# Transposing the second layer's sixteen softmax weights in SBUF: VectorE's 32x32 blocks and GpSimd copies

## The chip, the cores and the metric

The kernel runs on one core of a Trainium2 chip. The metric is the device time of one execution in microseconds (us), lower is better. Times are medians over several executions; where lines of a profile are shown, they come from one profiled execution.

## What is computed

The reference is an encoder trunk of two layers (DEPTH = 2) over 256 tokens of 2048 channels, all in float32. Each layer has a mixer and a gated feed-forward part with a short convolution. The mixer projects the normalised input to the q, k, v of two attention branches of eight heads each, head size 128. Branch A is attention with a window of +-128 tokens, two key/value groups and a learned sink; branch B is attention over neighbours in a 64-wide token grid with a learned bias table. What matters here is, for each of the sixteen heads of a layer:

```python
s = jnp.einsum('bnqgrd,bnkgd->bgrnqk', qb, kw) * (HEAD_DIM ** -0.5)   # scores (mask and sink, or bias, follow)
p = jnp.exp(s - m)
p = p / (jnp.sum(p, axis=-1, keepdims=True) + jnp.exp(snk - m))       # softmax weights
o = jnp.einsum('bgrnqk,bnkgd->bnqgrd', p, vw)                        # weights times values
```

The weights p of one head are a matrix of 256 queries by 256 keys. The scores come out with the queries on the 128 partitions (two tiles t of 128 queries); the product with the values needs the keys on the partitions (two tiles of 128 keys). So p has to be transposed between the softmax and the product.

## The kernel before, in words

**The weight stream.** Nearly all of TensorE's time goes into products with weight matrices. Each layer's weights are one long stream of 128x128 blocks, in units of 16 (1 MB). `unit_steps` (L319 on) loads a unit by a DMA of SP into one of four `raw` buffers, then splits it in two halves of 8 blocks: ScalarE casts to a rounded high part (L336), VectorE subtracts for the low part (L337), into one of four `hl` buffers. TensorE multiplies each block three times: high by high, high by low, low by high (L355 to L357 with features on the partitions, L418 to L420 with tokens on the partitions). The values and p are split in the same way by `split` (L427 on: cast at L430, subtract at L431).

**What runs beside it.** At the end of each unit `Stream.tick` calls `bg.tick`, which advances background jobs by a rate in steps per unit, and `plan`, which issues the loads and reductions (L231, L232) for the modulation of later parts. The attention of a layer is such a job: `attention()` keeps a list of live heads; each step advances every live head by one stage and then starts the next head, if its q, k and v are ready. The rate is `ATT[l]` from the end of the third group of the input projection, and in layer 1 `ATT_B[1]` = 0.4 from the end of branch A's output projection. `attended(HA)`, ahead of that projection, and `bg.finish(job)`, ahead of branch B's, run what is left at once.

**A head.** `head_a` and `head_b` start a head: q and k are split in halves in layer 1 (`SCORES_3`), and branch B takes a buffer p and loads the head's bias into it (SP, L889). `attend` (L643 on) is the rest, a stage up to each `yield`: the score matmuls (L648), the mask or bias addition with the row maximum (L651, into p), the exponential and the scaling (L659, L667); then the transpose and the split into pT, which has one buffer; then the product po with the values (L697) and its split into the head's output (L699, L700). The buffers p are two.

**The transpose, in two ways.** `rows` is None in layer 0 and in layer 1's branch A: TensorE transposes four 128x128 tiles into PSUM (L689) and `split` reads them there. In layer 1's branch B (`MOVED[1]` = (0, 8)) `turned_blocks` is called: VectorE transposes the 32x32 blocks of each query tile within themselves (L313), four DMAs of GpSimd for each tile put the blocks in their places in DRAM (L316), and two DMAs of SP read the transposed matrix back (L299), over the q and k of the head, which nobody needs any more. The reads are queued some units later (`BACK`), behind a VectorE instruction of the stream (`halved`, a dependency by hand). Two empty stages give all this time, so such a head has six stages and the others have four.

Instructions are issued in an order that a scheduler works out when the program is built, with the program's order as priority; an engine then takes them strictly in that order.

Of the kernel before, what the change touches and what calls it, by code (L numbers as in the profile page):

```python
# [9 lines left out]
F32 = mybir.dt.float32  # L10
F32R = mybir.dt.float32r
AF = mybir.ActivationFunctionType
ALU = mybir.AluOpType
AX = mybir.AxisListType

P = 128
# [10 lines left out]
EPS = 1e-6  # L27
NEG = -1e30
SCALE = HEAD ** -0.5
BEHIND = mybir.DependencyInfo(mybir.DependencyClass.Sync, mybir.DependencyReason.DATA)  # L30
GRID_W, NA_KH, NA_KW = 64, 8, 16
BLOCK = 32

# [46 lines left out]

H_RATE = [2.7, 1.7]

ATT = [1.288, 0.4]
ATT_B = [0.21, 0.4]

SCORES_3 = (1,)

BACK = [3, 4]
MOVED = [(0, 0), (0, 8)]

ADA_ORDER = [[p * KC + k for k in range(KC) for p in ps] for ps in ((0, 1), (2,), (3, 4), (5,))]
ADA_ORDER = [i for part in ADA_ORDER for i in part]
# [47 lines left out]
def encoder(ctx: ExitStack, tc: tile.TileContext, a: dict, out: bass.AP):  # L140
# [16 lines left out]
    sm = pool("sm", 3)  # L157
    mm = pool("mm", 4, space=bass.MemoryType.PSUM)
    ax = pool("ax", 3, space=bass.MemoryType.PSUM)
    dram = pool("dram", 2, space=bass.MemoryType.DRAM)  # L160

    ident = const.tile([P, P], F32, name="ident")
    make_identity(nc, ident[:])
# [43 lines left out]
    def paired(dt, name):  # L207

        t = ev.tile([P, 2 * S + ROW], dt, name=name, tag="u", bufs=2)
        return t[:, ROW - OFF : ROW - OFF + 2 * S].rearrange("p (a s) -> p a s", a=2)  # L210
# [71 lines left out]
                pass  # L282

    bg = Paced()
    halved = [None]

    def once(fn):

        due = [fn]

        def run():
            if due:
                due.pop()()

        return run

    def read_back(dst, src):

        tc.add_manual_dep(nc.sync.dma_start(dst, src).ins, halved[0], BEHIND)  # L299

    def later(n, fn):

        if n == 0:
            fn()
        else:
            bg.defer(lambda: later(n - 1, fn))

    def turned_blocks(p, rows, n, tag):

        y = dram.tile([P, n, S], F32, name=tag, tag=tag)  # L310
        to = y[:].rearrange("(b i) n (t a j) -> t a i n b j", i=BLOCK, t=2, a=P // BLOCK)
        for t, row in enumerate(rows):
            nc.vector.transpose(out=row, in_=p[t])  # L313
            src = row.rearrange("p (n b j) -> p n b j", n=n, j=BLOCK)
            for a in range(P // BLOCK):
                nc.gpsimd.dma_start(to[t, a], src[a * BLOCK : (a + 1) * BLOCK])  # L316
        return y

    def unit_steps(l, u, by_halves=False):  # L319

        raw = rawp.tile([P, UB * P], F32, name=f"w{l}_{u}", tag="raw")
        if not by_halves:
            nc.sync.dma_start(raw[:], a["ws"][l, u])
        halves = []
        streamed = any(m == "w_in" and mo < GATE_A // P for m, _, mo in STREAMS[l][u * UB : (u + 1) * UB])
        at = OFF if streamed else 0
        for j in range(2):
            n = UB * P // 2  # L330
            hl = hlp.tile([P, 2 * n + ROW], F32R, name=f"hl{l}_{u}_{j}", tag="hl")
            hl = hl[:, at : at + 2 * n].rearrange("p (a n) -> p a n", a=2)
            r = raw[:, j * n : (j + 1) * n]
            if by_halves:
                nc.sync.dma_start(r, a["ws"][l, u][:, j * n : (j + 1) * n])
            nc.scalar.copy(hl[:, 0], r)  # L336
            halved[0] = nc.vector.tensor_tensor(  # L337
                out=hl[:, 1], in0=r, in1=hl[:, 0].bitcast(F32), op=ALU.subtract
            ).ins.name
            halves.append(hl)  # L340
            if j == 0:
                yield halves
# [300 lines left out]
    def attend(q, k, v, p, mask, scale, sink, o, rows=None):  # L643

        sc = ax.tile([P, 2, S], F32, name="sc", tag="ax")
        for t in range(2):
            for i, j in by(q):
                nc.tensor.matmul(sc[:, t], q[i][:, t * P : (t + 1) * P], k[j], start=i + j == 0, stop=(i, j) == by(q)[-1])  # L648
        m = sm.tile([P, 2], F32, name="m", tag="m")
        for t in range(2):  # L650
            nc.vector.tensor_tensor_reduce(  # L651
                out=p[:, t], in0=sc[:, t], in1=mask[:, t], scale=scale, scalar=-3.0e38 if sink is None else sink,
                op0=ALU.add, op1=ALU.max, accum_out=m[:, t : t + 1],
            )
        nm = sm.tile([P, 2], F32, name="nm", tag="nm")
        nc.vector.tensor_scalar(out=nm[:], in0=m[:], scalar1=-1.0, scalar2=None, op0=ALU.mult)
        den = sm.tile([P, 2], F32, name="den", tag="den")
        for t in range(2):
            nc.scalar.activation(out=p[:, t], in_=p[:, t], func=AF.Exp, bias=nm[:, t : t + 1], accum_out=den[:, t : t + 1])  # L659
        if sink is not None:  # L660
            es = sm.tile([P, 2], F32, name="es", tag="es")
            nc.scalar.activation(out=es[:], in_=nm[:], func=AF.Exp, bias=sink)
            nc.vector.tensor_tensor(out=den[:], in0=den[:], in1=es[:], op=ALU.add)
        ri = sm.tile([P, 2], F32, name="ri", tag="ri")
        nc.vector.reciprocal(out=ri[:], in_=den[:])
        for t in range(2):
            nc.scalar.activation(out=p[:, t], in_=p[:, t], func=AF.Copy, scale=ri[:, t : t + 1])  # L667
        yield
        if rows is not None:
            rows = rows()  # L670
            y = turned_blocks([p[:, t] for t in range(2)], rows, 2, "pY")

            def back():
                for k in range(2):
                    read_back(rows[k], y[:, k])

            back = once(back)
            later(BACK[sink is None], back)
            yield
            yield  # L680
            back()
            pT = at.tile([P, 2, 2, S], F32R, name="pT", tag="pT", bufs=1)
            for k in range(2):
                split(pT[:, :, k], rows[k])
        else:
            tp = ax.tile([P, 2, S], F32, name="tp", tag="ax")
            for k in range(2):
                for t in range(2):
                    nc.tensor.transpose(tp[:, k, t * P : (t + 1) * P], p[:, t, k * P : (k + 1) * P], ident[:])  # L689
            pT = at.tile([P, 2, 2, S], F32R, name="pT", tag="pT", bufs=1)  # L690
            split(pT, tp[:])
        v = v()
        yield
        po = ax.tile([P, 512], F32, name="po", tag="ax")
        for i, j in by(v):
            for b in range(2):
                nc.tensor.matmul(po[:, :S], v[i][:, b], pT[:, j, b], start=i + j + b == 0, stop=i + b == 2)  # L697
        o = o()
        nc.scalar.copy(o[:, 0], po[:, :S])  # L699
        nc.vector.tensor_tensor(out=o[:, 1], in0=po[:, :S], in1=o[:, 0].bitcast(F32), op=ALU.subtract)  # L700
# [115 lines left out]
    for l in range(L):  # L816
# [41 lines left out]
        def head_a(i):  # L858
            g = i // (HA // GA)
            if i >= 6:  # L860
                oA.append(paired(F32R, f"oA{l}_{i}"))
            elif i % 2 == 0:
                o = place(("y0", "y1", "y2")[i // 2], 4, F32R, f"oA{l}_{i}")
                oA.extend((o[:, :2], o[:, 2:]))
            q = in_halves(qTa[:, i], f"qA{l}_{i}", "qh", l in SCORES_3)
            if i % (HA // GA) == 0:
                kvs[0] = in_halves(kTa[:, g], f"kA{l}_{g}", "kh", l in SCORES_3)
            k = kvs[0]
            yield
            p = at.tile([P, 2, S], F32, name="p", tag="p")  # L870

            def v():
                if i % (HA // GA) == 0:
                    kvs[1] = in_halves(packs[0][:, 1:4:2, g * HEAD : (g + 1) * HEAD], f"vA{l}_{g}", "vh", True)
                return kvs[1]

            def rows():
                spare = ev.tile([P, S], F32, name=f"spare{l}_{i}", tag="r", bufs=2)
                return [qTa[:, i], spare[:]]

            yield from attend(
                q, k, v, p, tables[0], SCALE, sink[:, i : i + 1], lambda: oA[i], rows if i < MOVED[l][0] else None
            )

        def head_b(hb):
            b, i = packs[1 + hb // 4], hb % 4
            v = b[:, 4:8].rearrange("p (t a) s -> p t (a s)", t=2)
            p = at.tile([P, 2, S], F32, name="p", tag="p")
            nc.sync.dma_start(p[:], a["bias"][l, hb])  # L889
            q = in_halves(b[:, 8 + i], f"qB{l}_{hb}", "qh", l in SCORES_3)  # L890
            k = in_halves(b[:, i], f"kB{l}_{hb}", "kh", l in SCORES_3)
            yield
            yield from attend(
                q, k, lambda: in_halves(v[:, :, i * HEAD : (i + 1) * HEAD], f"vB{l}_{hb}", "vh", True), p, p, 1.0, None,
                lambda: oB_of(hb), (lambda: [b[:, 8 + i], b[:, i]]) if hb < MOVED[l][1] else None,
            )

        def oB_of(hb):
# [314 lines left out]
```

## Time and profile before

| | |
|---|---|
| median of 3 runs | 2661.03 us (2660.66 to 2664.07) |
| profiled execution | 2661.44 us |
| its span, first to last instruction | 2659.3 us |
| busy: TensorE, VectorE, ScalarE, GpSimd | 2647.6, 2106.2, 1411.5, 75.0 us |
| DMA | 704.63 MB, mean 265 GB/s |

Busy time counts an engine's instructions, without the time in which it waits or issues DMAs. TensorE's matmuls overlap one another, so their single durations add up to more than the time they take: it is better to look at the distance from start to start, or at the chain of work that ended last. Two layers follow one another; layer 1's attention lies at about 1500 to 1800 us. In the profile's lines `ps_t` is the output of a product with tokens on the partitions, `ps` of one with features on the partitions, `tp` the transposed p in PSUM, `pY` the matrix in DRAM.

### The profile page before, as it was taken

The numbers are of one execution on the slowest core, as the hardware profiler recorded it, in microseconds if no ns is written. First come the engines' busy times: TensorE is split into PE (matmuls) and PEld (weight loads), VectorE is DVE, ScalarE is ACT, GpSimd is POOL, SyncE is SP. The second block draws the span as 40 slices with busy tenths as digits, with TensorE's granted clock in tenths as the row PEclk, the third lists the DMA queues.
The fourth block names the chain that finished last, engine by engine and source line by source line (L and its number), as shares of the span: only waits on it lengthen the run. The fifth ranks groups of instructions, "written<-read, shape, count | busy, mean of one in ns | idle before, by whom it ended". The sixth has DMA issues, their size and how long they took to land.

```text
span 2659.3 us, 50973 instructions
## 1 busy us (share of the span) xinstructions
PE 2647.6 (100%) x21224; PEld 2562.6 (96%) x21224; DVE 2106.2 (79%) x2983; ACT 1411.5 (53%) x2292; POOL 75.0 (3%) x89
## 2 busy tenths in 40 slices
PE   9999999999999999999999999999999999999999
PEld 7888899999999999999998889999999999999999
DVE  8898998997987888788876666868888866655664
ACT  5445865456653554355554566555565445544553
POOL 0001100000000000000000001310000000000000
PEclk9999999999999999999999999999999999999999
DMA  9987789885777778788756666877747765555554
GB/s 365 349 327 297 264 300 351 321 311 212 290 295 286 296 290 287 288 297 296 295 205 256 236 229 238 299 264 261 278 179 287 297 251 191 191 197 194 196 191 143
DMA packets 106394, 704.63 MB, mean 265 GB/s; under 512 B 14001, under 2 KB 18353, under 8 KB 22321
## 3 DMA queue, kind: packets, MB, share of 16 engines
q1 hardware_dynamic: 104114, 699.27, 71.6%
q8 instruction: 166, 2.72, 0.4%
q0 software_dynamic: 2048, 2.10, 0.3%
q14 instruction: 66, 0.54, 0.1%
HBM read 697.13 MB, written 4.19 MB: 264 GB/s over the span
## 4 chain that ended last, share of the span: by engine, by line
PE 90%; DVE 5%; DMA 2%; ACT 1%; issue 1%; POOL 0%; DVEq 0%; ACTq 0%
PE ps L355 25%; PE ps L357 25%; PE ps L356 25%; PE ps_t L420 4%; PE ps_t L418 4%; PE ps_t L419 4%; DVE hl L337 2%; DVE aw L232 1%; DMA aw<-in_aw 1%; PE sc L648 1%; PE po L697 1%; ACT hl L336 1%; PE tp L689 0%; PE qtp L621 0%; DMA w<-in_ws 0%
## 5 line engine op out<-in xcount | busy, mean ns | idle before, releaser
L337 DVE TENSOR_TENSOR hl<-w,hl 128x1024 fp32r<-128x1024 f32 x928 | 1128.4, 1222 | 338.7 <-ACT hl L336 332.1
L336 ACT CAST hl<-w 128x1024 fp32r<-128x1024 f32 x928 | 970.6, 1049 | 738.3 <-PE ps L357 509.5
L355 PE MATMUL ps<-h,hl 128*128 128x256 f32 x3328 | 923.9, 278 | 1.3 <-DVE ya L979 0.6
L356 PE MATMUL ps<-h,hl 128*128 128x256 f32 x3328 | 921.1, 277 | 0.0
L357 PE MATMUL ps<-h,hl 128*128 128x256 f32 x3328 | 920.9, 277 | 0.0
L355 PEld LDWEIGHTS ps<-h,hl 128*128 128x128 f32 x3328 | 625.0, 188 | 2.4 <-DVE ya L979 0.8
L356 PEld LDWEIGHTS ps<-h,hl 128*128 128x128 f32 x3328 | 625.6, 188 | 0.4
L357 PEld LDWEIGHTS ps<-h,hl 128*128 128x128 f32 x3328 | 624.6, 188 | 0.0
L232 DVE CUSTOM_DVE_ANT_0 aw<-aw,cact,ab 128x2048 f32<-128x2048 f32 x189 | 443.5, 2347 | 61.1 <-DMA aw<-in_aw 60.4
L418 PE MATMUL ps_t<-hl,h 128*128 128x512 f32 x576 | 223.5, 393 | 2.1 <-ACT h L510 1.6
L419 PE MATMUL ps_t<-hl,h 128*128 128x512 f32 x576 | 225.1, 391 | 0.4
L420 PE MATMUL ps_t<-hl,h 128*128 128x512 f32 x576 | 224.6, 391 | 0.0
L1058 DVE SCALAR_TENSOR_TENSOR u<-ps,cw,u 128x255 f32<-128x255 f32 x304 | 146.2, 481 | 66.5 <-ACT u L1056 62.5
L1056 ACT ACTIVATE u<-ps,cw 128x256 f32<-128x256 f32 x152 | 85.7, 564 | 183.1 <-PE ps L357 183.0
L357 PE MATMUL ps<-merged,hl 128*128 128x256 f32 x512 | 141.8, 277 | 0.2 <-DVE hl L337 0.2
L355 PE MATMUL ps<-merged,hl 128*128 128x256 f32 x512 | 141.7, 277 | 0.0
L356 PE MATMUL ps<-merged,hl 128*128 128x256 f32 x512 | 141.7, 277 | 0.0
L356 PE MATMUL ps<-act_o,hl 128*128 128x256 f32 x512 | 141.6, 277 | 0.0
L357 PE MATMUL ps<-act_o,hl 128*128 128x256 f32 x512 | 141.6, 276 | 0.0
L355 PE MATMUL ps<-act_o,hl 128*128 128x256 f32 x512 | 141.4, 277 | 0.0
L418 PEld LDWEIGHTS ps_t<-hl,h 128*128 128x128 f32 x576 | 108.0, 188 | 25.5 <-ACT h L510 2.6
L419 PEld LDWEIGHTS ps_t<-hl,h 128*128 128x128 f32 x576 | 108.2, 188 | 24.0 <-DVE hl L337 2.1
(235 smaller groups left out, 4657.8 us busy)
## 6 DMA issues: line engine op xcount, KB each, us to landing
w<-in_ws SPq DMA_DIRECT2D x463, 1024.0 KB, 5.0
aw<-in_aw SPq DMA_DIRECT2D x189, 1024.0 KB, 6.1
p<-in_bias SPq DMA_DIRECT2D x16, 256.0 KB, 4.4
x<-in_xT SPq DMA_DIRECT2D x4, 512.0 KB, 5.5
aw_o<-in_aw SPq DMA_DIRECT2D x2, 1024.0 KB, 13.1
pY<-packB POOLq DMA_DIRECT2D x64, 32.0 KB, 4.2
packB<-pY SPq DMA_DIRECT2D x16, 128.0 KB, 2.7
out<-x SPq DMA_DIRECT2D x16, 128.0 KB, 2.6
```

The costliest lines, as they stand in the source:

```text
L232: nc.vector.tensor_tensor_reduce(out=raw[:], in0=raw[:], in1=cact[:], scale=1.0, scalar=ab[:, i : i + 1], op0=ALU.mult, op1=ALU.add, accum ...
L336: nc.scalar.copy(hl[:, 0], r)
L337: halved[0] = nc.vector.tensor_tensor(out=hl[:, 1], in0=r, in1=hl[:, 0].bitcast(F32), op=ALU.subtract).ins.name
L355: nc.tensor.matmul(out, hi, act[0], start=first, stop=False)
L356: nc.tensor.matmul(ps[:, :S], hi, act[1], start=False, stop=False)
L357: nc.tensor.matmul(out, lo, act[0], start=False, stop=last)
L418: nc.tensor.matmul(ps[:], xh, hi, start=kc == kcs[0], stop=False)
L419: nc.tensor.matmul(ps[:], xh, lo, start=False, stop=False)
L420: nc.tensor.matmul(ps[:], xl, hi, start=False, stop=kc == kcs[-1])
L648: nc.tensor.matmul(sc[:, t], q[i][:, t * P : (t + 1) * P], k[j], start=i + j == 0, stop=(i, j) == by(q)[-1])
L1056: nc.scalar.activation(out=u, in_=ps, func=AF.Identity, scale=w[:, 1:2], bias=w[:, 3:4])
L1058: nc.vector.scalar_tensor_tensor(out=u[:, to], in0=ps[:, of], scalar=w[:, j : j + 1], in1=u[:, to], op0=ALU.mult, op1=ALU.add)
```

## The change

In layer 1 all sixteen heads now go through `turned_blocks`, and it no longer uses DRAM. VectorE transposes the 32x32 blocks of both query tiles in one instruction (128 x 512), from p into `rows`. Then sixteen copies by GpSimd, each of 32 partitions by 2 x 2 x 32 elements, take the blocks from partition group b to partition group a, back into p, which then holds the transposed matrix. `split` reads it from p in one cast and one subtract of 512 elements, as it reads PSUM in layer 0. The stages that a head waits between the copies and the split are `STEPS` (one for each branch), so each head of layer 1 has five stages. For branch A `rows` is the q of this head and of the one before it (for head 0 a spare buffer), for branch B the head's k and q as before. The rate of layer 1's attention goes from 0.4 to 0.43 steps a unit (`ATT`). The DRAM buffers, the read-backs, `BACK`, `once` and the dependency by hand go. Layer 0 keeps TensorE's transposes.

```diff
-ATT = [1.288, 0.4]
+ATT = [1.288, 0.43]
...
-BACK = [3, 4]
-MOVED = [(0, 0), (0, 8)]
+MOVED = [(0,0), (8,8)]
+STEPS = [1, 1]
...
-    def turned_blocks(p, rows, n, tag):
-
-        y = dram.tile([P, n, S], F32, name=tag, tag=tag)
-        to = y[:].rearrange("(b i) n (t a j) -> t a i n b j", i=BLOCK, t=2, a=P // BLOCK)
-        for t, row in enumerate(rows):
-            nc.vector.transpose(out=row, in_=p[t])
-            src = row.rearrange("p (n b j) -> p n b j", n=n, j=BLOCK)
-            for a in range(P // BLOCK):
-                nc.gpsimd.dma_start(to[t, a], src[a * BLOCK : (a + 1) * BLOCK])
-        return y
+    def turned_blocks(src, rows, n):
+
+        nc.vector.transpose(out=rows, in_=src)
+        blocks = rows.rearrange("p t (n k) -> p n t k", n=n)
+        dst = src.rearrange("p t (n k) -> p (t n k)", n=n).rearrange("p (n t k) -> p n t k", n=n, t=2)
+        for b in range(0, P, BLOCK):
+            for a in range(0, P, BLOCK):
+                nc.gpsimd.tensor_copy(
+                    out=dst[a : a + BLOCK, :, :, b : b + BLOCK], in_=blocks[b : b + BLOCK, :, :, a : a + BLOCK]
+                )
...
         if rows is not None:
-            rows = rows()
-            y = turned_blocks([p[:, t] for t in range(2)], rows, 2, "pY")
-
-            def back():
-                for k in range(2):
-                    read_back(rows[k], y[:, k])
-
-            back = once(back)
-            later(BACK[sink is None], back)
-            yield
-            yield
-            back()
-            pT = at.tile([P, 2, 2, S], F32R, name="pT", tag="pT", bufs=1)
-            for k in range(2):
-                split(pT[:, :, k], rows[k])
+            turned_blocks(p[:], rows(), 2)
+            for _ in range(STEPS[sink is None]):
+                yield
+            tp = p
         else:
...
-            pT = at.tile([P, 2, 2, S], F32R, name="pT", tag="pT", bufs=1)
-            split(pT, tp[:])
+        pT = at.tile([P, 2, 2, S], F32R, name="pT", tag="pT", bufs=1)
+        split(pT, tp[:])
...
             def rows():
-                spare = ev.tile([P, S], F32, name=f"spare{l}_{i}", tag="r", bufs=2)
-                return [qTa[:, i], spare[:]]
+                return qTa[:, i - 1 : i + 1] if i else paired(F32, f"spare{l}")
...
-                lambda: oB_of(hb), (lambda: [b[:, 8 + i], b[:, i]]) if hb < MOVED[l][1] else None,
+                lambda: oB_of(hb), (lambda: b[:, i : 9 + i : 8]) if hb < MOVED[l][1] else None,
```

More of the change, by code (lines that the diff above doesn't have):

```diff
@@ L29 @@
 SCALE = HEAD ** -0.5
-BEHIND = mybir.DependencyInfo(mybir.DependencyClass.Sync, mybir.DependencyReason.DATA)
 GRID_W, NA_KH, NA_KW = 64, 8, 16
@@ L159, in encoder @@
     ax = pool("ax", 3, space=bass.MemoryType.PSUM)
-    dram = pool("dram", 2, space=bass.MemoryType.DRAM)
     ident = const.tile([P, P], F32, name="ident")
@@ L284, in encoder @@
     bg = Paced()
[L285 to L299, printed above, removed]
     def later(n, fn):
@@ L336, in unit_steps @@
             nc.scalar.copy(hl[:, 0], r)
-            halved[0] = nc.vector.tensor_tensor(
-                out=hl[:, 1], in0=r, in1=hl[:, 0].bitcast(F32), op=ALU.subtract
-            ).ins.name
+            nc.vector.tensor_tensor(out=hl[:, 1], in0=r, in1=hl[:, 0].bitcast(F32), op=ALU.subtract)
             halves.append(hl)
```

## The prediction

> **What bounds the kernel now.** I read the page first: the span, the busy times, the chain that ended last.
>
> ```profile
> span 2659.3 us, 50973 instructions
> ...
> PE 2647.6 (100%) x21224; PEld 2562.6 (96%) x21224; DVE 2106.2 (79%) x2983; ACT 1411.5 (53%) x2292; POOL 75.0 (3%) x89
> ...
> PE 90%; DVE 5%; DMA 2%; ACT 1%; issue 1%; POOL 0%; DVEq 0%; ACTq 0%
> ```
>
> TensorE is busy all the time and 90% of the chain. A busy TensorE need not be dense, so I went on to the windows of the second layer's attention (branch A about 1500 to 1640 us, branch B 1640 to 1760) and to TensorE's waits from 1400 to 1850 us, where the only one listed is this:
>
> ```profile
> 1500.00:1640.00 140.00, 139.94 (x814) 123.02 (x813) 95.47 (x161) 90.56 (x199) 4.91 (x3) 1.00 0.64 234
> 1640.00:1760.00 120.00, 120.00 (x1053) 120.00 (x1053) 93.85 (x169) 70.02 (x132) 39.37 (x64) 1.00 0.80 279
> ```
> ```profile
> PEld tp L689 <- ACT packB L622: 0.3, 1, 0.3
> ```
>
> The columns after the length are TensorE, weight loads, VectorE, ScalarE, GpSimd, granted clock, DMA share and GB/s. TensorE has no stall to give back here beyond 0.3 us, also in branch B, where the weights go through DRAM. The clock is full. So the change gains only what it takes off TensorE, and loses only what makes TensorE wait.
>
> How much lateness of VectorE and ScalarE stays unseen? Two rows of TensorE's timeline, 24 matmuls apart, and ScalarE's rows for branch A:
>
> ```profile
> 1628.79 0.28 PE L357 MATMUL ps<-h,hl 128*128 128x256 f32 x1
> ...
> 1631.51 0.28 PE L357 MATMUL ps<-h,hl 128*128 128x256 f32 x1
> ```
> ```profile
> L336 ACT CAST hl<-w 128x1024 fp32r<-128x1024 f32 x44 | 45.9, 1046 | 35.8 <-PE ps_t L420 32.5 <-PE ps L357 3.3
> ```
>
> Half a unit of weights (8 blocks, 24 matmuls) lasts 2.72 us. ScalarE idles 35.8 us before the casts because TensorE has not yet freed an hl buffer: there are four. A freed buffer is wanted again three halves later (8.2 us); refilling it takes 1.05 us on ScalarE and 1.22 us on VectorE (L337, below). So the weights lead by an estimated 5.9 us, and a hold-up shorter than that costs nothing.
>
> **What goes from TensorE.** In branch A of layer 1, eight heads times four transposes:
>
> ```profile
> L689 PE MATMUL tp<-ident,p x32: 270/272/327, 1519.2 to 1634.2; 128*128 128x128 f32 x32
> ```
> ```profile
> 1569.55 0.44 PE tp L689 x4
> ...
> 1633.78 0.66 PE tp L689 x4
> ```
>
> The 272 ns overlap one another; in the chain a group of four costs 0.44 us, and 0.66 us only where it also waited for ScalarE. 8 x 0.44 = **3.5 us**; the upper bound is 8 x 0.66 + 0.3 = 5.6 us, the lower 8 x 0.27 = 2.2 us, if of each group only one transpose counted. I take 3.5, since seven of the eight groups stand in the chain with 0.44. Branch B has none of these (its eight heads go by DRAM already), so it gains nothing on TensorE.
>
> **VectorE and ScalarE.** By line, for the two windows:
>
> ```profile
> L337 DVE TENSOR_TENSOR hl<-w,hl 128x1024 fp32r<-128x1024 f32 x45 | 54.4, 1223 | 28.4 <-ACT hl L336 28.3
> L232 DVE CUSTOM_DVE_ANT_0 aw<-aw,cact,ab 128x2048 f32<-128x2048 f32 x7 | 16.4, 2349 | 6.1 <-DMA aw<-in_aw 6.1
> ...
> L431 DVE TENSOR_TENSOR pT<-tp,pT 128x512 fp32r<-128x512 f32 x8 | 5.5, 684 | 0.1
> ...
> L431 DVE TENSOR_TENSOR qA<-packA,qA 128x256 fp32r<-128x256 f32 x7 | 3.0, 422 | 0.0
> ```
> ```profile
> L337 DVE TENSOR_TENSOR hl<-w,hl 128x1024 fp32r<-128x1024 f32 x41 | 50.0, 1221 | 19.6 <-ACT hl L336 15.5 <-PE sc L648 4.0
> L232 DVE CUSTOM_DVE_ANT_0 aw<-aw,cact,ab 128x2048 f32<-128x2048 f32 x7 | 16.4, 2342 | 1.3 <-DMA aw<-in_aw 1.2
> ...
> L313 DVE STREAM_TRANSPOSE packB<-p 128x256 f32<-128x256 f32 x16 | 6.4, 430 | 1.7 <-ACT p L667 1.7
> ...
> L431 DVE TENSOR_TENSOR pT<-packB,pT 128x256 fp32r<-128x256 f32 x12 | 4.5, 419 | 0.0
> L431 DVE TENSOR_TENSOR qB<-packB,qB 128x256 fp32r<-128x256 f32 x6 | 2.5, 423 | 0.0
> L431 DVE TENSOR_TENSOR vB<-packB,vB 128x256 fp32r<-128x256 f32 x6 | 2.5, 420 | 0.0
> L431 DVE TENSOR_TENSOR kB<-packB,kB 128x256 fp32r<-128x256 f32 x6 | 2.5, 419 | 0.0
> ```
>
> 256 more elements cost 0.684 - 0.419 = 0.27 us, so a block transpose of 512 is an estimated 0.43 + 0.27 = 0.70 us. Branch A gains eight: 5.6 us over 140 in which VectorE is 68% busy (95.47); the idle time before L337 hides them. Branch B replaces 2 x 0.43 by 0.70 and, in the subtract into pT, 2 x 0.42 by about 0.68: 0.3 us less a head. ScalarE:
>
> ```profile
> L430 ACT CAST pT<-packB x16: 406/417/420, 1662.9 to 1783.2; 128x256 fp32r<-128x256 f32 x16
> L430 ACT CAST pT<-tp x8: 577/592/616, 1520.4 to 1634.5; 128x512 fp32r<-128x512 f32 x8
> ```
>
> One cast of 512 replaces one in branch A (0.59 us, now from SBUF) and two of 256 in branch B (0.83): nothing, or 0.2 us less a head, on an engine at 65% and 58%. All of it is off the path: 0.
>
> **GpSimd.** It loses 64 DMA issues and gets 16 heads x 16 copies of 32 partitions x 128 elements. No copy of this kind is in the trace. The nearest rows:
>
> ```profile
> L316 POOL DMA_DIRECT2D pY<-packB x64 | 39.4, 618 | 96.6 <-DVE packB L313 51.8 <-issue 44.4
> ...
> masks.py:199 POOL TENSOR_SCALAR_AFFINE_SELECT ident<-ident 128x128 f32<-128x128 f32 x1 | 0.3, 292 | 0.1
> masks.py:197 POOL MEMSET ident<- 128x128 f32 x1 | 0.2, 204 | 0.3 <-POOLq L1205 0.3
> ```
>
> The select reads and writes 128 elements a partition, as a copy does, so I take its 0.29 us: 4.7 us a head. Bounds: 0.20 (the memset, which reads nothing) and 0.62 us (a DMA issue), 3.3 to 9.9 us a head.
>
> Time for them: the 32 transposes of L689 span 115 us for eight heads, 16.4 us a head at 0.4 steps a unit (2.5 units), so 15.2 us at 0.43. In branch B the score matmuls lie
>
> ```profile
> 1634.56 0.77 PE sc L648 x6
> ...
> 1735.63 0.68 PE sc L648 x6
> ```
>
> seven heads apart: 14.4 us each. Between the block transposes, which follow the softmax, and the split stand two or three units, and pT has one buffer, which the head before frees only with its own po. So 4.7 us fit, even stretched to 10.
>
> The fifth stage that branch A gets (four before) needs the higher rate: head 7 starts about unit 41 of the layer instead of 43 and ends at 51 instead of 50; line `attended(HA)` forces the rest only at 52. Nothing is forced: 0.
>
> **VectorE against GpSimd.** The trace has one clear meeting of the two, first GpSimd's power, once disturbed and once not, then VectorE's timeline:
>
> ```profile
> 259.13 4.08 POOL L482 TENSOR_TENSOR qrs<-qss,mhalf 128x8 f32<-128x8 f32 x1 [8.03 <-DVE qss L481]
> ...
> 1563.45 1.64 POOL L482 TENSOR_TENSOR qrs<-qss,mhalf 128x8 f32<-128x8 f32 x1 [26.63 <-DVE qss L481]
> ```
> ```profile
> 258.96 0.29 DVE L613 TENSOR_TENSOR qn<-rt 128x128 f32<-128x128 f32 x1
> ...
> 259.36 2.36 DVE L337 TENSOR_TENSOR hl<-w,hl 128x1024 fp32r<-128x1024 f32 x2
> 261.63 1.29 DVE L949 TENSOR_TENSOR packB<-ps_t,packB 128x512 f32<-128x512 f32 x2
> ```
>
> The power ends at 263.21, 1.58 us after VectorE's last instruction with both inputs in SBUF gave way to one that reads PSUM: GpSimd stood still for 2.5 us, and the two L337 lasted 2.36 us, as always. So copies pass between VectorE's two-SBUF-input instructions. These (L337, L232, qA) fill 73.8 of 140 us in branch A, with the new subtract from SBUF 8.7 of 15.2 us a head, which leaves 6.5 us, 0.41 a copy. In branch B (L337, L232, pT, qB, vB, kB) they fill 78.4 of 120, 9.4 of 14.4 us a head: 5.0 left, **0.31 a copy**. At 0.29 it fits, narrowly in branch B.
>
> The Trainium skill, "SBUF — State Buffer", section "Who interferes with whom", says that a VectorE instruction with two SBUF inputs contends with a GpSimd instruction that reads SBUF, and that the second to issue blocks until the first ends; the row at 259.13 agrees on GpSimd's side, and no row shows VectorE held. The skill's "GPSIMD Engine Reference", section 3.1, gives about 1.8 cycles an element at 1.2 GHz in a good loop, by which a copy would be an estimated 0.19 us and a head 3.1 us; no run here shows it, and the sum would be the same.
>
> **DMA queues.** The 64 stores and 16 read-backs go, with SP's wait on them: nothing waits for SP that TensorE feels, so 0. But p now lives until the split, and there are two p buffers. A branch-B head loads its bias into p when it starts, and adds the scores to it one step later. So far the load waits for the block transposes of the head two before; now it waits for that head's split, which stands in the very step of the addition:
>
> ```profile
> SPq L889 <- DVE packB L313: 18.7, 5, 5.6
> ```
> ```profile
> DMA to landing us min/median/max: 2.4/4.0/5.5
> ```
>
> (The second row is from p's own view, layer 1: from a bias load's issue to its landing.) Behind it on SP stand the weight loads, with four raw buffers (some 22 us) ahead; behind the mask addition that wants it on VectorE stand L337s, with 5.9 us. A load of 4.0 us fits into that, and the head's own block transposes aren't due before the next step: 0.
>
> **Sum.** The profiled execution took 2661.44 us (span 2659.3 and 2.1 around it), 0.4 above the median of 2661.03. 2661.4 - 3.5 = **2657.9**, less 0.13%. About 0.2% (5.3 us) is what a measurement of this kernel can tell from no change, so this counts as within.
>
> **The rivals.**
> - *The copies run into VectorE (slower).* For: 0.31 us of room a copy in branch B against 0.29. Against: VectorE wasn't held in the one meeting. It decides from 0.31 us in branch B, 0.41 in A. At 0.45, midway between the select and the DMA issue, 16 copies are 7.2 us: B overruns by 9.4 + 7.2 - 14.4 = 2.2, A by 0.7; eight heads each: 23 - 3.5, so 2681. At 0.62 it is about 2723. Chance 0.22.
> - *The bias comes late.* For: VectorE takes its instructions in order, and the addition stands close behind the split that lets the load go. If it waits for the whole landing and the subtracts of pT, qB, kB and vB (0.68 + 3 x 0.42 = 1.9 us) stand with it, the lead of 5.9 us just covers a landing of 4.0 us and is 1.5 us short at 5.5; four of the eight heads at 5.5 cost 6 us, so 2664. Against: other work can be put between split and addition. Chance 0.12.
> - *Nothing is gained*, since the new order of VectorE's work costs the 3.5 us elsewhere: 2661.4. Chance 0.05.
> - *All of the transposes' waits go too*, by the upper bound 5.6 us: 2655.8 or less. Chance 0.04.
>
> **How the numbers follow.** The forecast has 0.57. Within 0.2%: 0.57 + 0.12 + 0.05 = 0.74; slower 0.22; faster 0.04. The range starts at 2656, just above the best case, and ends at 2674, a copy of 0.42 us (B overruns by 1.7, A by 0.2, 8 x 1.9 - 3.5 = 12); above it I leave out the worse half of the first rival.
>
> **What would show it.** Right: no tp in layer 1; TensorE's waits from 1480 to 1800 us still under 1 us; copies at 0.2 to 0.3 us each, a head's sixteen done within 10 us; L337 at 1.22 us. Wrong: po or ps waiting for VectorE or ScalarE there; a pT cast waiting for GpSimd; a mask addition waiting for the bias for over 3 us; L337 longer than 1.3 us, which would mean that GpSimd holds VectorE.

## The result, and the profile after

The changed kernel takes 2659.41 us (median of 22 executions, 2656.18 to 2663.97) against 2664.14 us for the kernel before, run beside it (22, 2660.66 to 2676.13): ratio 0.998, 95% interval 0.9972 to 0.9988, that is 3.2 to 7.5 us less. The forecast, 3.5 us less (0.9987), lies inside; as a time it was 2657.9 us, 1.5 below the median. In three later comparisons the kernel before took 2661.0, 2660.9 and 2661.5 us, so part of the 4.7 us between the medians is scatter.

Where that scatter is, and what the change does without it, two rows of TensorE show. The first is the first matmul of layer 1 with tokens on the partitions, ahead of all attention work; the second is the first matmul of the output projection, behind it. The column with "to" has the first and the last start in the window. From the kernel before, views of ps_t and merged:

```profile
L418 PE MATMUL ps_t<-hl,h x288: 388/390/508, 1395.3 to 1607.3; 128*128 128x512 f32 x144
```
```profile
L355 PE MATMUL ps<-merged,hl x256: 275/277/287, 1842.8 to 1930.0; 128*128 128x256 f32 x128
```

The same from the changed kernel, where the lines are 19 lower:

```profile
L399 PE MATMUL ps_t<-hl,h x288: 389/389/478, 1398.1 to 1606.6; 128*128 128x512 f32 x144
```
```profile
L336 PE MATMUL ps<-merged,hl x256: 274/276/286, 1842.2 to 1929.5; 128*128 128x256 f32 x128
```

This stage lasted 447.5 us before and lasts 444.1 after: **3.4 us less**. Ahead of it the two profiled executions differ by 2.8 us the other way, in code that is the same; over the traces below with the same code up to there, the stage begins between 1393.4 and 1398.1 us. Behind the stage, from the first start of `merged` to the end of the span, both take 816.5 us (2659.3 - 1842.8 and 2658.7 - 1842.2), and so do the traces below, one of them 817.5. The four traces, this one and three below, in which layer 1 has sixteen copies a head for all its heads and the rate is 0.43 agree in the stage within 0.7 us (443.7 to 444.4). So the scatter between the traces lies mostly ahead of the stage, and I compare the kernels by this stage, each time of one profiled execution, as well as by their medians.

The page, and the two windows of the attention:

```profile
span 2658.7 us, 51010 instructions
...
PE 2646.4 (100%) x21192; PEld 2561.3 (96%) x21192; DVE 2116.5 (80%) x2975; ACT 1407.9 (53%) x2284; POOL 194.0 (7%) x281
...
PE 88%; DVE 5%; POOL 2%; ACT 2%; DMA 1%; issue 1%; DVEq 0%; ACTq 0%; POOLq 0%
```
```profile
1500.00:1640.00 140.00, 139.56 (x799) 122.25 (x798) 106.95 (x179) 91.26 (x202) 90.32 (x145) 1.00 0.65 235
1640.00:1760.00 120.00, 120.00 (x1054) 120.00 (x1053) 97.77 (x156) 70.47 (x132) 71.33 (x115) 1.00 0.70 257
```

TensorE has 32 instructions fewer (21192 against 21224). GpSimd goes from 4.91 to 90.32 us busy in branch A's window, VectorE from 95.47 to 106.95. TensorE's waits from 1480 to 1800 us are again a single one:

```profile
PE sc L629 <- ACT packB L603: 0.4, 1, 0.4
```

The copies by tile (shortest, median and longest in ns), then by group (busy us, mean ns, idle time before):

```profile
L298 POOL COPY p<-packB x128: 285/293/2408, 1634.0 to 1748.6; 32x128 f32<-32x128 f32 x128
L298 POOL COPY p<-packA x112: 281/292/2423, 1530.4 to 1632.5; 32x128 f32<-32x128 f32 x112
```
```profile
L298 POOL COPY p<-packB 32x128 f32<-32x128 f32 x128 | 76.8, 600 | 39.3 <-DVE packB L293 23.9 <-issue 10.4
L298 POOL COPY p<-packA 32x128 f32<-32x128 f32 x112 | 72.4, 646 | 34.5 <-DVE packA L293 18.1 <-issue 11.2 <-DVE qss L462 0.8
```

A copy by itself takes 0.29 us, as the select did. The mean is twice that, and the longest are as long as VectorE's reductions (2.4 us): a copy that meets VectorE with two SBUF inputs stands until that instruction is done. In the trace 109 of the 256 copies took longer than 0.35 us; each of these ends within 0.17 us of the end of such an instruction, and none of the other 147 lies inside one. VectorE pays little, as its timeline and groups in branch B show:

```profile
1680.03 0.51 DVE L412 TENSOR_TENSOR vB<-packB,vB 128x256 fp32r<-128x256 f32 x1
1680.46 0.51 DVE L412 TENSOR_TENSOR qB<-packB,qB 128x256 fp32r<-128x256 f32 x1
1680.89 0.51 DVE L412 TENSOR_TENSOR kB<-packB,kB 128x256 fp32r<-128x256 f32 x1
```
```profile
L320 DVE TENSOR_TENSOR hl<-w,hl 128x1024 fp32r<-128x1024 f32 x41 | 51.1, 1255 | 12.6 <-ACT hl L319 11.1 <-PE sc L629 1.5
```

A subtract of 256 that took 0.42 us takes 0.51 among copies, the weight subtract 1.255 us against 1.221 in the mean.

### The profile page after: what moved, and what is told of

Its sections match the earlier page's. It is cut to its first block, busy times and chain, and to the rows that moved or that the text cites. A ratio compares the mean times of both kernels' runs of the same rounds, so it can differ in the third digit from the quotient of the medians.

```text
span 2658.7 us, 51010 instructions
## 1 busy us (share of the span) xinstructions
PE 2646.4 (100%) x21192; PEld 2561.3 (96%) x21192; DVE 2116.5 (80%) x2975; ACT 1407.9 (53%) x2284; POOL 194.0 (7%) x281
## 4 chain that ended last, share of the span: by engine, by line
PE 88%; DVE 5%; POOL 2%; ACT 2%; DMA 1%; issue 1%; DVEq 0%; ACTq 0%; POOLq 0%
PE ps L336 26%; PE ps L338 26%; PE ps L337 26%; PE ps_t L401 3%; PE ps_t L400 3%; PE ps_t L399 3%; POOL p L298 2%; DVE hl L320 2%; DMA aw<-in_aw 1%; DVE aw L230 1%; ACT hl L319 1%; PE sc L629 1%; PE po L667 1%; POOL qrs L463 0%; ACT qsq L569 0%
## 6 DMA issues: line engine op xcount, KB each, us to landing
aw_o<-in_aw SPq DMA_DIRECT2D x2, 1024.0 KB, 12.5
```

## Experiments

Each run's times are medians of 4 to 11 executions, with the ratio to the kernel before on the same chip and its 95% interval. "Stage" is the stretch of the first section in the one execution that was profiled, 447.5 us before and 444.1 after. The last column is the stage's difference from before.

| run | us | ratio | stage, us | against before |
|---|---|---|---|---|
| all sixteen heads on TensorE | 2664.43 | 1.0012 (1.0003 to 1.002) | 451.3 | +3.8 |
| branch A alone by copies | 2660.87 | 0.9998 (0.9989 to 1.0007) | 448.5 | +1.0 |
| branch B alone by copies | 2661.30 | 0.9997 (0.9988 to 1.0006) | 447.5 | 0.0 |
| copies twice (32 a head) | 2715.97 | 1.0202 (1.0188 to 1.0216) | 502.6 | +55.1 |
| a memset ahead of each copy | 2676.45 | 1.006 (1.0047 to 1.0074) | 463.4 | +15.9 |
| 24 copies a head | 2678.28 | 1.0068 (1.0052 to 1.0083) | 462.5 | +15.0 |
| rate 0.4 | 2669.47 | 1.0032 (1.002 to 1.0043) | 456.0 | +8.5 |
| rate 0.4, power off GpSimd | 2659.32 | 0.9992 (0.9983 to 1.0001) | 445.0 | -2.5 |
| power off GpSimd | 2660.91 | 0.9997 (0.9988 to 1.0006) | 443.7 | -3.8 |
| 24 copies, power off GpSimd | 2666.84 | 1.0017 (1.0009 to 1.0026) | 450.0 | +2.5 |
| layer 0's branch B too | 2669.24 | 1.0032 (1.0019 to 1.0044) | 444.4 | -3.1 |
| layer 0's last four heads too | 2659.41 | 0.9993 (0.9984 to 1.0002) | 444.1 | -3.4 |

### What leaves TensorE, or what leaves DRAM

Theory T is the prediction's: the gain is the 0.44 us of TensorE's transposes for each head. Rival D: dropping DRAM, its small transfers and SP's waits brings it.

All on TensorE:

```diff
-ATT = [1.288, 0.43]
+ATT = [1.288, 0.4]
...
-MOVED = [(0,0), (8,8)]
+MOVED = [(0,0), (0,0)]
```

> All sixteen heads of layer 1 back on TensorE (64 transposes, no copies, no DRAM, rate 0.4). Theory T, the gain is what leaves TensorE, 0.44 us a head: eight heads more than before, +3.5 us against before (ratio 1.0013), and layer 1's attention 7.0 us longer than in the changed kernel. Rival D, the gain came from dropping DRAM, its small transfers and SP's waits, and the transposes cost nothing: -4.7 us (0.998), as fast as the changed kernel.

Branch A alone:

```diff
-MOVED = [(0,0), (8,8)]
+MOVED = [(0,0), (8,0)]
```

> Branch A's eight heads by blocks and copies, branch B's eight on TensorE, no DRAM. T: eight heads on TensorE as before, so 0 us (1.0000); the stages move: branch A 3.5 us shorter, branch B 3.5 us longer. D: -4.7 us (0.998).

Branch B alone:

```diff
-ATT = [1.288, 0.43]
+ATT = [1.288, 0.4]
...
-MOVED = [(0,0), (8,8)]
+MOVED = [(0,0), (0,8)]
```

> Branch B's eight heads by blocks and copies in place of DRAM, branch A's on TensorE as before, rate 0.4. T: the same work on TensorE as before, 0 us (1.0000). D: all of the gain, -4.7 us (0.998).

Measured: +3.4, -0.1 and +0.3 us in the medians. Between all on TensorE and none, the stage shortens from 451.3 to 444.1 us: 7.2 us for sixteen heads, 0.45 a head, against the 0.44 of the chain. With branch B taken from DRAM to copies and nothing else, the time stays what it was. D falls. Branch A alone has 1.0 us more in the stage than before, where T has 0; one wait of TensorE of 0.6 us (its first transposes in branch B, for ScalarE) is in it, and the rest isn't explained. What the medians of the result show beyond 3.5 us isn't explained by any of this; the stage has nothing of it.

### How many copies would be too many

```diff
+                for _ in range(2):
-                nc.gpsimd.tensor_copy(
+                    nc.gpsimd.tensor_copy(
...
```

> The changed kernel with every GpSimd copy issued twice in a row (32 a head; the second writes the same values). My room sum of the prediction: 32 x 0.29 = 9.3 us a head in gaps of 6.5 (A) and 5.0 (B): short by 2.8 and 4.3 us a head, 57 us, so +53 against before (1.020). Rival G, a copy passes at each boundary between VectorE's instructions and holds VectorE for 0.1 us at most: VectorE loses 3 us a head more, inside its idle time, but a head's copies last 17 to 25 us, longer than the 15.2 us between heads, so heads back up and TensorE waits at po: +10 to +70 us, with GpSimd busy without a break and L320 still under 1.4 us. Rival N, still hidden: -3.5 to -5 us.

Measured: +55 us. The room sum of the prediction said +53, and that is chance: it has 22 us of it in branch A and 34 in B, and the trace has 35 in the units up to branch A's end and 20 behind. Its waits, from 1480 to 1860 us, ScalarE's, VectorE's and then TensorE's:

```profile
ACT p L641 <- DVE nm L638: 62.5, 15, 14.4
ACT pT L412 <- POOL p L299: 57.1, 12, 10.5
```
```profile
DVE pT L413 <- ACT pT L412: 45.3, 10, 9.3
...
DVE packA L293 <- POOL p L299: 24.1, 4, 6.9
DVE qn L579 <- POOL qrs L464: 21.3, 4, 11.5
```
```profile
PE ps_t L401 <- DVE hl L321: 18.6, 5, 8.1
PE ps L339 <- DVE hl L321: 5.9, 5, 3.0
```

ScalarE stands at the cast into pT until the head's last copy has landed, up to 10.5 us, and takes no weight cast in that time; VectorE's subtract for the low part, and TensorE, come late with it. Not all of it starts there: ScalarE waits as long for the softmax (`nm`, the row maximum) from a VectorE that itself stands for the copies (`packA`) and for GpSimd's power (`qrs`, of which more below). How the loss divides among these waits this run doesn't tell. The rival G named this direction, though the longest waits are in front of the split and of the softmax and not at po.

The waits aren't the whole loss either. TensorE stands idle for 39.7 us of the stage, which is 58.5 us longer than in the changed kernel. After the longer stalls it also runs slower for a while. Behind the one of 8.1 us, at 1577.8 us, ten weight loads in a row take 0.32 to 0.33 us each, where 0.19 is usual, and the granted clock of this slice (the number behind GpSimd's) is 0.74, where the kernels before and after have 1.00 in all slices from 1480 to 1800 us:

```profile
1580.00:1600.00 20.00, 14.04 (x63) 11.77 (x64) 15.22 (x30) 6.28 (x14) 7.97 (x17) 0.74 0.50 180
```

Such stretches add up to 32 us in the stage. `ps_t` matmuls start 0.43 us apart in them and 0.23 us elsewhere, so they cost an estimated 15 us more. With 24 copies (granted clock down to 0.87 in a slice of 20 us) and at rate 0.4 (0.91), below, the same happens: a stall of TensorE costs more than its length.

Which part of a GpSimd instruction counts, the reading or the time? The next kernel adds as many instructions that read nothing:

```diff
+                nc.gpsimd.memset(dst[a : a + BLOCK, :, :, b : b + BLOCK], 0.0)
                 nc.gpsimd.tensor_copy(
...
```

> The changed kernel with a GpSimd memset of each destination block (32 x 128 elements, written and not read) ahead of its copy: as many GpSimd instructions as with the copies doubled (+55 us), but the added ones read no SBUF. Theory R, GpSimd stands still only where it has to read while VectorE reads two SBUF inputs: the memsets last about 0.2 us also under VectorE's subtracts, a head takes 10.5 + 16 x 0.24 = some 14 us, and the kernel loses at most 10 us against the changed one (0.998 to 1.002 of before). Rival I, any GpSimd instruction stands still there: memsets stretched to 1.2 and 2.3 us like the copies, and +40 to +55 us.

Its memsets by line, then its copies and memsets by group:

```profile
L298 POOL MEMSET p<- x256: 195/198/203, 1507.4 to 1773.5; 32x128 f32 x128
```
```profile
L299 POOL COPY p<-packB 32x128 f32<-32x128 f32 x128 | 81.8, 639 | 6.6
L299 POOL COPY p<-packA 32x128 f32<-32x128 f32 x112 | 63.4, 566 | 5.8
L298 POOL MEMSET p<- 32x128 f32 x256 | 50.8, 198 | 61.6 <-DVE packA L293 18.1 <-DVE spare L293 16.0 <-issue 9.5
```

No memset of 256 took longer than 0.203 us, while copies go on being stretched: only reading stands still, as R says. But the kernel loses 15.5 us against before, 19 in the stage against the changed kernel, where R had 10 at most. Some 3 to 4 us more a head on GpSimd (16 x 0.2 and their issue) are dear whatever they do. Here too VectorE stands for the power, 13.9 us in three waits of branch A, the longest 9.1; this kernel wasn't run without the power, so how much of its loss goes by that queue stays open.

Next, 24 copies a head:

```diff
+                for _ in range(1 + (a // BLOCK) % 2):
-                nc.gpsimd.tensor_copy(
+                    nc.gpsimd.tensor_copy(
...
```

> The changed kernel with every second copy issued twice: 24 a head. Room sum: 24 x 0.29 = 7.0 us, short by 0.5 us a head in branch A and 2.0 in B, 20 us, so +16 against before (1.006). Rival Q, what decides is ScalarE, which waits in its queue for the copies ahead of weight casts that TensorE needs 6 us later: 24 copies at 0.65 us take 16 us a head against 15.2 and 14.4 between heads, ScalarE waits for GpSimd before most pT casts but mostly under 6 us: +5 to +12 against before (1.002 to 1.0045), more of it in branch A, where the doubled copies cost 35 of 55 us.

Measured: +17 us, by chance again near the room sum (+16), and again in the wrong place: of the stage's 15.0 us nothing lies behind branch A (from unit 52 of the layer on it is as long as in the changed kernel, 184.2 us), where the sum had 16 of its 20. Q falls too: it had 5 to 12. What costs, the next runs show.

### GpSimd's other work

Leaving branch A's rate at 0.4 was to show that the rate is no part of the gain:

```diff
-ATT = [1.288, 0.43]
+ATT = [1.288, 0.4]
```

> The changed kernel with branch A's rate left at 0.4 steps a unit. Counted through the generator, head 7's last stage then falls into unit 53 and is forced at 52, half a unit early: nothing waits, -3.5 to -4.7 us against before as with the change (0.998 to 0.9987). Rival: the forced stage makes TensorE wait for the copies and the split, 3 to 10 us, and the higher rate is a part of the gain (1.000 to 1.003).

Measured: +8.5 us; this expectation was wrong, and the rival's place for it, the forced stage at unit 52, was wrong for most of it: the longest stall of TensorE (2.6 us, at 1584.3 us, for a copy of ScalarE's that `sc` needs) is at about unit 40. GpSimd's timeline there, then VectorE's, then ScalarE's:

```profile
1562.46 7.14 POOL L298 COPY p<-packA 32x128 f32<-32x128 f32 x16 [1.43 <-DVE packA L293]
1569.69 1.64 POOL L463 TENSOR_TENSOR qrs<-qss,mhalf 128x8 f32<-128x8 f32 x1
```
```profile
1571.36 1.29 DVE L578 TENSOR_TENSOR qn<-ps_t,qrs 128x512 f32<-128x512 f32 x2 [4.37 <-POOL qrs L463]
```
```profile
1572.39 1.04 ACT L319 CAST hl<-w 128x1024 fp32r<-128x1024 f32 x1 [1.85 <-PE ps_t L401]
1580.77 0.51 ACT L640 ACTIVATE p<-p,nm 128x256 f32<-128x256 f32 x1 [7.33 <-DVE nm L637]
...
1583.35 1.98 ACT L319 CAST hl<-w 128x1024 fp32r<-128x1024 f32 x2
```

Read it from the top. GpSimd also raises the q and k norms to the power -0.5 (L463). Here that power is queued behind a head's sixteen copies. VectorE, in order, stands 4.37 us at the product that needs it; behind that product stand weight subtracts, a reduction of the modulation and the next head's softmax. ScalarE waits 7.33 us for that softmax, and behind its exponential stand weight casts: from 1573.4 to 1583.4 us none is made, and the lead of some 6 us is gone. The copy for `sc` stands behind those casts.

To test this the power goes off GpSimd, and a reciprocal on VectorE stands in its place:

```diff
-        nc.gpsimd.tensor_tensor(out=dst, in0=src, in1=mhalf[:, :k], op=ALU.pow)
+        nc.vector.reciprocal(out=dst, in_=src)
```

with the rate at 0.4,

> The kernel with branch A's rate at 0.4 (+8.5 us against before, 12 to 13 more than the changed one), with the power that ends the q and k norms taken off GpSimd: a reciprocal on VectorE stands in its place, so q and k are divided by their mean square and not by its root. Theory P, most of the 12 us is the power queued behind sixteen copies, VectorE waiting for it in its order (15.8 us in branch A, the longest 5.7), and ScalarE and TensorE behind: the stalls at units 28 to 46 go, some 8 us, and what the forced stage costs at units 49 to 53, some 3.5 us, stays: 0 to +1 us against before (1.000). Rival F, the loss is that of the rate and the forced stage: still +8 us (1.003).

with the rate at 0.43, as a control,

> The changed kernel (rate 0.43) with the same reciprocal on VectorE in place of GpSimd's power: q and k are divided by their mean square. P: VectorE's 6.8 us of waits for the power in branch A go, but TensorE had no stall there, so the time is that of the changed kernel, -3.5 to -4.7 us against before (0.998 to 0.9987). Rival: the waits cost TensorE something after all, -6 us or less (0.9975).

and with 24 copies a head:

> 24 copies a head (+18 us against before) with the reciprocal on VectorE in place of GpSimd's power: q and k are divided by their mean square. If the power's queue is what makes the copies dear in branch A (13.8 us of VectorE's waits, the longest 8.5), the loss falls to 5 to 10 us (1.002 to 1.004). If it is ScalarE's wait for the copies in front of the weight casts, it stays within 3 us of +18 (1.006 to 1.008).

At rate 0.4 the stage falls from 456.0 to 445.0 us and the median to 2659.3: 11 of the 12 us were the power's queue (I had expected 8; 10.3 lie in the units up to branch A's end), and what is left for the forced stage is about 1. The control's stage, 443.7 us, is the changed kernel's within 0.4, so moving the power gains nothing where TensorE had no stall. Its median misses: only 0.5 us below before (95% interval from 3.2 less to 1.6 more), where 3.5 to 4.7 were expected, with executions from 2657.6 to 2665.6 us. The control thus rests on the stage. With 24 copies the median is 5.4 us above before, in the range for the power's queue, and the stage falls from 462.5 to 450.0 us: 12.5 of the 18.4 us over the changed kernel were the power, too. VectorE's waits from 1500 to 1640 us with 24 copies, the power on GpSimd and then off it:

```profile
DVE qn L579 <- POOL qrs L464: 13.8, 3, 8.5
DVE packA L293 <- POOL p L299: 13.3, 4, 4.2
```
```profile
DVE packA L293 <- POOL p L299: 15.8, 5, 4.2
DVE pT L413 <- ACT pT L412: 6.6, 1, 6.6
```

What is left, 6 us, goes with waits for the copies themselves, VectorE's at the block transpose, which writes q buffers that the head before still has to be copied from, and ScalarE's at the split; no run takes these two apart.

### Layer 0

```diff
-MOVED = [(0,0), (8,8)]
+MOVED = [(0,8), (8,8)]
...
-            bg.pace(job, 0.36)
+            bg.pace(job, 0.42)
```

> The changed kernel with layer 0's branch B (eight heads) by blocks and copies too, and its rate 0.42 in place of 0.36 for the fifth stage. Theory T alone: another 3.5 us off TensorE, -7 to -8 us against before (0.997). Rival V, there VectorE is 95% busy in the trace of before (19.06 of 20 us at 340 to 360 us) and reads two SBUF inputs in some four fifths of the time: the copies get about 3 us of gaps a head and else one copy at each boundary, ScalarE waits for them, TensorE stalls: +5 to +30 us against the changed kernel (1.000 to 1.009 of before).

Measured: +8.3 us against before. Layer 1's stage is as short as with the change (444.4), but begins at 1407.7 us. V is right; VectorE has no wait for a power in this stretch, so that queue isn't the cause here. TensorE's and ScalarE's waits from 280 to 460 us:

```profile
PE ps L338 <- DVE hl L320: 4.8, 4, 1.6
PE po L667 <- ACT pT L411: 4.8, 1, 4.8
```
```profile
ACT pT L411 <- POOL p L298: 17.3, 5, 5.4
```

The last four of these heads alone:

```diff
-MOVED = [(0,0), (8,8)]
+MOVED = [(0,4), (8,0)]
...
-                lambda: oB_of(hb), (lambda: b[:, i : 9 + i : 8]) if hb < MOVED[l][1] else None,
+                lambda: oB_of(hb), (lambda: b[:, i : 9 + i : 8]) if hb >= MOVED[l][1] else None,
...
-            bg.pace(job, 0.36)
+            bg.pace(job, 0.4)
```

> The changed kernel with the last four heads of layer 0's branch B by blocks and copies too, at a rate of 0.4 there. All eight cost 11 us more than the changed kernel, with the stalls where layer 0's heads follow one another closely (units 53 to 63 of it) and little at units 70 to 99. If the stalls come with the early heads alone, the four late ones take 1.7 us off TensorE: -5 to -6.5 us against before (0.9978). If a VectorE that is 95% busy is enough, each head costs about 1.3 us net: 0 to +2 us (1.000).

Measured: -2 us against before, between the two expectations and no better than the change. From unit 48 to unit 84 of layer 0, which holds these heads, the trace has 229.7 us, the changed kernel 230.0 and the kernel before, with the same code there, 229.5: of the 1.75 us that leave TensorE nothing arrives that stands out from scatter. The trace shows no wait of TensorE that would explain it; the cause stays open. No run is clearly faster than the changed kernel.

## Why the prediction was right, point by point

- **What bounds.** Right: TensorE had nothing to give back, and branch B without DRAM gains nothing (0.0 in the stage).
- **What goes from TensorE.** Right in kind and size: 3.5 us forecast, 3.4 in the stage, 0.45 us a head against 0.44. The absolute time came within 1.5 us, but before's own medians differ by 3 us from comparison to comparison, so that is partly luck; the stage is the better evidence.
- **VectorE and ScalarE, off the path.** Right in effect. The block transpose took 0.71 us (0.70 forecast), the cast from SBUF 0.62. The subtract into pT took 0.74 and not 0.68, among copies.
- **GpSimd's copies.** The price was right, 0.29 us. A head's sixteen were to be done within 10 us; they took 7.7 to 14.4 us (that one with a power between them), nine of the sixteen heads over 10. The signs that I named as wrong came in part: ScalarE did wait for GpSimd, once, at the first head, for 5.8 us, about as long as the lead that I had estimated (5.9), and TensorE didn't feel it. At rate 0.4 a wait of 7.3 us (for the softmax) did reach TensorE.

```profile
ACT pT L411 <- POOL p L298: 5.8, 1, 5.8
```

- **VectorE against GpSimd.** This step failed, though it didn't touch the sum. "0.31 a copy" of room was to decide. In the runs VectorE isn't displaced by the copies: at a boundary between two of its instructions one copy passes, for which VectorE pays about 0.1 us (0.42 to 0.51, and 1.227 to 1.351 at most), and the copies wait for the rest. What decides is how late a head's copies, and the powers behind them, are against what waits for them in order. The Trainium skill, "SBUF — State Buffer", section "Who interferes with whom", says that VectorE with two SBUF inputs contends with a GpSimd instruction that reads SBUF and not with one that only writes; the memsets agree (0.203 us at most, where copies went to 2.4). It also says, in full for VectorE's two-port modes, that the second to issue blocks until the first ends; that held for the copies, while VectorE's longest weight subtract was 1.351 us against 1.227 before, a loss shorter than a copy.
- **GpSimd's queue.** Left out. The prediction counted GpSimd's copies and forgot its powers behind them; in the changed kernel they keep VectorE for 6.8 us in branch A (below, second row), where the kernel before had 5.4 in as many waits (first row), and TensorE doesn't feel it. At rate 0.4 it is 15.8 us, the longest 5.7, and costs 11 us. So "nothing is forced: 0" was right for rate 0.43, but by luck: what the rate decided is where the powers fall among the copies, and the prediction hadn't looked at that.

```profile
DVE qn L597 <- POOL qrs L482: 5.4, 3, 1.8
```
```profile
DVE qn L578 <- POOL qrs L463: 6.8, 3, 3.1
```

- **DMA queues and the late bias.** Right: SP's bias loads wait for the split now (10.2 us in eight waits), and VectorE felt 0.9 us of it:

```profile
DVE p L632 <- DMA p<-in_bias: 0.9, 2, 0.7
```

- **The slower rival.** It had the right engines and the wrong mechanism. Its sum at 0.62 us a copy gives 2724 and not 2723, which changes nothing. Its price at twice the copies came out within 2 us, by errors that cancel.

## What to carry to other kernels

In layer 1, where TensorE is dense, work taken off it came back one for one, as the chain prices it (0.44 us for four transposes), but only while every queue that took the work over kept its lead. Before giving an idle engine a burst, list what else that engine does and who waits for it in order: here three powers of 1.6 us in branch A, each behind a head's copies (7 us in the one shown), cost some 10 us, through VectorE and ScalarE, with GpSimd at half load. An idle engine's average says nothing of it; try the change with the burst half as long again and see what breaks.

## What the runs showed of the hardware

A GpSimd copy of 32 partitions by 128 float32 took 0.28 to 0.29 us undisturbed, and a memset of the same block 0.198; the copy was held under VectorE's two-SBUF-input instructions for up to 2.4 us and the memset never. VectorE's block transpose of 128 x 512, one SBUF input, took 0.71 us; in the changed kernel no copy ran beside it, and with 24 and 32 copies, where some did, it took 0.69 to 0.72. Behind a stall of TensorE of 8.1 us the granted clock was lower for some us (0.74 in a slice of 20 us, weight loads at 0.33 us in place of 0.19), and then full again.
